# Turning the merged activations with VectorE blocks and transfers through memory, in place of TensorE turns

## The chip, the cores and the metric

The kernel runs on one core of a Trainium2 chip. The metric is device time in microseconds (us) for one execution. The core has five engines with a queue each: TensorE (PE in the profile) multiplies matrices, VectorE (DVE) and ScalarE (ACT) work elementwise, GpSimd (POOL) here does little but issue transfers, and SyncE (SP) issues the transfers of weights. Sixteen DMA engines, shared by all queues, move data between device memory and the on-chip buffer of 128 partitions. TensorE writes its results to eight accumulator banks of 128 x 512 float32.

## What is computed

One layer of a diffusion backbone over 256 tokens of 2048 features, with a prefix of 256 context tokens. The part that the change touches is the merge of two branches ahead of the output projection:

```python
def gated_merge(y_conv, y_hgrn, p_gc, p_gh, w_o):
    return (jax.nn.sigmoid(p_gc) * y_conv + jax.nn.sigmoid(p_gh) * y_hgrn) @ w_o
```

`y_conv` is a convolution branch times its pointwise weights `w_pw` (1024 x 2048), `y_hgrn` a recurrent branch times `hgrn_out_w` (1024 x 2048), and `w_o` is 2048 x 2048. Before this come a modulation, a normalisation and the input projections; behind it a normalisation, the residual and an MLP with a squared ReLU (2048 to 8192 to 2048). All of it is float32.

## The kernel before

**Products in three terms.** A float32 operand is split into a high part `hi` (rounded to the faster matmul type, `F32R`) and a low part `lo = x - hi`. A product is the sum of `hi*hi`, `hi*lo` and `lo*hi`, so three matmuls (`mm3r`, line 256, recorded at line 185). ScalarE makes the high part and VectorE the low part: lines 123 and 126 for weights, line 237 (`split`) for activations.

**The stream of weights.** `Stream` (line 52) loads tiles of 128 x 1024 (512 KB) from the SyncE queue into one of five raw buffers (`RAWS`), and prepares each (lines 123 and 126) up to four tiles (`AHEAD`) before TensorE uses it. A raw buffer is free again when VectorE has made the low part. Between the weight tiles run tiles of another product (`gemv`, line 1226): one VectorE operation, `gacc`, per tile, from the same raw buffers. In this part of the kernel one such tile goes with every two weight tiles.

**The token-major projections.** `tokens` (line 277) computes an output with tokens on partitions. Its output of 256 tokens x 2048 features is made in two groups of 1024 features, each with four accumulators: `tb` (two blocks of 128 tokens) by `j` (two blocks of 512 features). A group runs over the input features in steps `k` of 128; each step uses one weight tile and 12 matmuls. The last three steps of a group (`LAST`) are done accumulator by accumulator, so that the accumulators finish one after another, and after that each is evacuated. With `pairs=True` the order of accumulators is (tb 0, j 0), (1, 0), (0, 1), (1, 1). `pre(g, k)` is called ahead of each step of a group outside those last three.

**Around the merge.** Line 824 projects the recurrent branch (weights `who`, 8 steps in each group). Line 857 projects the convolution branch (weights `wpw`, 8 steps per group); this is "pw" below. Its evacuation `ev_pw` (line 828) merges, per token block `tb` and per block `c` of 512 features, the accumulator with the gates and the other branch: a multiplication (line 830) and an addition (line 831), both on VectorE. The merged values lie in `gp[0]`, with tokens on partitions.

The output projection (line 974, weights `wo`, 16 steps in each of two groups; "wo" below) needs them with features on partitions, as high and low part: pages `zh` and `zl`, page `c` for the features 512c to 512c + 511, in the order feature block, token. `turn_z` (line 833) makes them from 32 turns of 128 x 128 on TensorE (line 840, a transpose against an identity matrix), four to a bank, and after every four one split of the bank (128 x 512). Four of its eight steps run in pw's second group, two each at k = 3 and k = 4 (`pre_pw`); the other four in wo's first group, one each at k = 3 to 6 (`pre_wo`).

**Order.** The instructions of each engine run in the order of its queue. A scheduler fixes that order when the program is built: what stands earlier in the program has priority when it is ready, by the scheduler's own clock. `issue_after(ins)` puts instructions behind `ins` on the same engine, and nothing more; `his[-1]` and `los[-1]` are the weight splits prepared last.

**Pages.** Tiles of 128 x 1024 float32 come from one pool of 30 pages. A page is used again when its last reader is done, and an instruction that wants a new page waits for that. The loads of the residual input into `xr` (line 855, four pages of 512 KB on GpSimd's queue) and of the gain rows (lines 1276 and 1277, the same queue) take their pages from that pool, as do the gates `gp`, `zh`, `zl` and the pages of the branch activations.

Of the kernel before, what the change touches and what calls it, by code (L numbers as in the profile page):

```python
# [8 lines left out]
F32 = mybir.dt.float32  # L9
# [6 lines left out]
P = 128  # L16
T = 256
D = 2048
KT = D // P
# [7 lines left out]
TW = 1024  # L27
# [24 lines left out]
class Stream:  # L52


    def __init__(self, kn):
        self.kn = kn
        self.items = []
        self.done = 0
        self.behind = []
        self.ready = collections.deque()  # L60
        self.raws = collections.deque()
        self.dma = None
# [66 lines left out]
    def next(self, ahead=AHEAD):  # L129
        while len(self.ready) < ahead and self.done < len(self.items):  # L130
            self.prepare()
        while ahead > 1 and self.done < len(self.items) and self.items[self.done][1] is not None:
            self.prepare()
        return self.ready.popleft()


class Kernel:
    def __init__(self, ctx, tc, a, out):
        self.tc = tc
        self.nc = tc.nc  # L140
        self.a = a
        self.out = out
        self.wp = ctx.enter_context(tc.tile_pool(name="wp", bufs=1))
        self.pg = ctx.enter_context(tc.tile_pool(name="pg", bufs=1))
        self.sp = ctx.enter_context(tc.tile_pool(name="sp", bufs=1))
        self.cp = ctx.enter_context(tc.tile_pool(name="cp", bufs=1))
        self.ps = ctx.enter_context(tc.tile_pool(name="ps", bufs=1, space=bass.MemoryType.PSUM))
        self.bg = collections.deque()
        self.his, self.los = [], []
        self.credit = 0.0  # L150
        self.queued = None
# [213 lines left out]
    def run(self):  # L365
        nc, a = self.nc, self.a
# [3 lines left out]
        v = self.v  # L370
# [131 lines left out]
        for i in range(2):  # L502
            ps = self.bank()
# [160 lines left out]
        for c in range(8):  # L664
            part = sums(c, self.last3)
            ps = self.bank()
            for t in range(KP // 2):
                st.fetch_to(FETCH)
                w = st.whole()
                for k2 in range(2):  # L670
                    k = 2 * t + k2
                    g = 32 * (k % 4)
# [69 lines left out]
        for h in range(NH):  # L742
            accs = []
            for d in range(2 * (h > 0)):
                accs.append(self.bank())
                for hf in range(2):
                    hi, lo = st.next()
                    for k8 in range(8):
                        k = 8 * hf + k8
# [55 lines left out]
        gp = [[None] * 4, [None] * 4]  # L805
# [20 lines left out]
        zh, zl = self.pages(4, F32R, "zh"), self.pages(4, F32R, "zl")  # L826

        def ev_pw(tb, c, acc):
            z, y = self.cut(gp[0], tb, c), self.cut(gp[1], tb, c)
            nc.vector.tensor_tensor(z, acc, z, op=ALU.mult)  # L830
            nc.vector.tensor_tensor(z, z, y, op=ALU.add)

        def turn_z():

            for k in range(0, KT, 2):
                ps = self.bank()
                for j in range(2):
                    o = (k + j) % 8 * P
                    for tb in range(2):
                        nc.tensor.transpose(out=ps[:, j * T + tb * P:j * T + (tb + 1) * P], in_=gp[0][2 * tb + k // 8][:, o:o + P], identity=v["ident"])  # L840
                self.split(ps, self.at(zh, k, 2), self.at(zl, k, 2))
                yield
        zturn = turn_z()

        def pre_pw(g, k):
            for _ in range(2 * (g == 1 and k > 2)):
                next(zturn)

        def pre_wo(g, k):
            if g == 0 and 2 < k < 7:  # L850
                next(zturn)
            if g == 0 and 7 < k < 12:
                j = k - 8
                with self.tc.issue_after(self.los[-1].ins):
                    nc.gpsimd.dma_start(xr[j][:, :TW], a["x"][(j // 2) * P:(j // 2 + 1) * P, (j % 2) * TW:(j % 2 + 1) * TW])

        self.tokens(self.operand(self.cv), ev_pw, 1.3, nk=8, pairs=True, pre=pre_pw)


# [112 lines left out]
        hid = {}  # L972
        begun = self.first_up(yp, xr, A2, mv[:, 0], h2)
        self.tokens(zx, ev_wo, 1.4, end=True, pre=pre_wo, begin=begun)


# [243 lines left out]
    def warm(self, n=WARM):  # L1220

        ps = self.bank()
        for _ in range(n):
            self.pe(self.nc.tensor.matmul, ps[:, :P], self.ones_r, self.ones_r, start=True, stop=True)

    def gemv(self, raw, i, k, h):

        nc = self.nc
        if k == 0:
            self.accv = self.page(F32, "gacc")  # L1230
        acc = self.accv[:, :TW]
        s = self.sc[:, k:k + 1]
        if k == 0:
            nc.vector.tensor_scalar(out=acc, in0=raw, scalar1=s, scalar2=None, op0=ALU.mult)
        else:
            nc.vector.scalar_tensor_tensor(acc, raw, s, acc, op0=ALU.mult, op1=ALU.add)  # L1236
        if k == KT - 1:
            gen = self.gain_row(acc, i, h)
            self.bg.appendleft(gen)
            self.grow_gen[i, h] = gen  # L1240
# [383 lines left out]
```

## Time and profile before

| | |
|---|---|
| median of 3 runs | 1643.5 us (1642.47 to 1644.42) |
| the profiled execution, its own time | 1644.45 us |
| its span in the trace | 1642.7 us |
| memory read, written | 370.93 MB, 2.10 MB |
| granted clock of TensorE | full in all 40 slices |

The page lists busy time by engine, then 40 slices of the span, then the DMA queues, then the chain that ended last: the work followed back from the last instruction, at each step to whatever released it. What is on that chain sets the time; what is beside it has slack. Further views, asked of the same trace, are used below: the instructions of one line, the chain in order of time, busy times in chosen windows, a timeline of one engine, groups of instructions, and DMA issues. Times in the timeline and the chain are from the start of the span; pw runs at about 782 to 830 us, wo's first group from 830 us on.

### The profile page before, as it was taken

How to read it: one execution, taken by the hardware profiler on the slowest of the kernel's cores; microseconds unless marked ns; L12 is line 12 of the kernel's file. 1: busy time of each engine (PE TensorE's matmuls, PEld its weight loads, DVE VectorE, ACT ScalarE, POOL GpSimd, SP SyncE). 2: the span in 40 equal slices, each digit the busy share in tenths (PEclk: the TensorE clock that was granted, in tenths of full speed). 3: DMA queues.
4: the chain of work that ended last, by engine and by line, in shares of the span. 5: the costliest groups of instructions: out<-in, count | busy, mean ns of one | idle time of the engine just before them, and what ended most of it. 6: DMA issues, size and time to landing. Idle time of an engine off the chain costs nothing.

```text
span 1642.7 us, 22019 instructions
## 1 busy us (share of the span) xinstructions
PE 1627.8 (99%) x8211; PEld 1359.2 (83%) x8211; DVE 1163.1 (71%) x1703; ACT 799.9 (49%) x1142; POOL 8.1 (0%) x18
## 2 busy tenths in 40 slices
PE   8999999999999999999999999999999999999998
PEld 6668888888988888888888888888888888888887
DVE  7777777778868889967887766456655665566555
ACT  6553444443554444653446665445544554346543
POOL 0000000000000000000000000000000000000000
PEclk9999999999999999999999999999999999999999
DMA  9998954444656556688887376677667667666553
GB/s 375 389 395 292 318 163 149 154 142 141 204 185 227 189 187 210 228 277 294 317 291 269 136 233 204 212 237 240 219 205 232 233 214 215 232 219 195 190 192 116
DMA packets 103771, 374.47 MB, mean 228 GB/s; under 512 B 11632, under 2 KB 12400, under 8 KB 103664
## 3 DMA queue, kind: packets, MB, share of 16 engines
q1 hardware_dynamic: 102096, 368.60, 66.4%
q0 software_dynamic: 1280, 4.21, 0.9%
q8 instruction: 64, 1.05, 0.3%
q14 instruction: 43, 0.35, 0.1%
q10 hardware_dynamic: 288, 0.26, 0.0%
HBM read 370.93 MB, written 2.10 MB: 227 GB/s over the span
## 4 chain that ended last, share of the span: by engine, by line
PE 93%; DVE 2%; DMA 2%; ACT 1%; issue 1%; SPq 0%; ACTq 0%; DVEq 0%
PE bank L185 62%; PE bank L252 18%; PE bank L254 9%; PE bank L1396 2%; DMA raw<-wpw 1%; DVE wlo L126 1%; DMA x<-ctx 1%; DMA rawpage<-wm 1%; ACT whi L123 0%; PE bank L1427 0%; PE bank L1438 0%; PE bank L1436 0%; DVE gacc L1236 0%; SPq L498 0%; PE bank L1419 0%
## 5 line engine op out<-in xcount | busy, mean ns | idle before, releaser
L126 DVE TENSOR_TENSOR wlo<-raw,whi 128x1024 fp32r<-128x1024 f32 x488 | 594.7, 1224 | 356.2 <-ACT whi L123 348.4
L123 ACT ACTIVATE whi<-raw 128x1024 fp32r<-128x1024 f32 x488 | 513.4, 1059 | 577.7 <-PE bank L185 322.9
L185 PE MATMUL bank<-whi,h 128*128 128x512 f32 x1264 | 396.6, 392 | 0.8 <-ACT h L629 0.5
L252 PE MATMUL bank<-h,whi 128*128 128x512 f32 x1280 | 322.4, 394 | 0.0
L185 PEld LDWEIGHTS bank<-whi,h 128*128 128x128 f32 x1264 | 237.3, 188 | 50.9 <-DVE h L1085 0.7
L252 PEld LDWEIGHTS bank<-h,whi 128*128 128x128 f32 x1280 | 230.7, 189 | 41.3
L185 PE MATMUL bank<-wlo,h 128*128 128x512 f32 x632 | 246.9, 391 | 0.7 <-DVE wlo L126 0.5
L185 PE MATMUL bank<-whi,hidh 128*128 128x512 f32 x503 | 195.3, 388 | 0.0
L185 PE MATMUL bank<-wlo,hidh 128*128 128x512 f32 x503 | 195.3, 388 | 0.0
L185 PE MATMUL bank<-whi,hidl 128*128 128x512 f32 x503 | 195.3, 388 | 0.0
L254 PEld LDWEIGHTS bank<-h,wlo 128*128 128x128 f32 x1280 | 174.6, 190 | 12.6
L254 PE MATMUL bank<-h,wlo 128*128 128x256 f32 x1280 | 178.5, 283 | 0.0
L185 PE MATMUL bank<-h,whi 128*128 128x512 f32 x512 | 164.7, 403 | 0.0
L185 PEld LDWEIGHTS bank<-wlo,h 128*128 128x128 f32 x632 | 118.8, 188 | 26.5 <-DVE wlo L126 2.4
L185 PEld LDWEIGHTS bank<-whi,hidh 128*128 128x128 f32 x503 | 94.5, 188 | 19.3
L185 PEld LDWEIGHTS bank<-whi,hidl 128*128 128x128 f32 x503 | 94.5, 188 | 19.2
L185 PEld LDWEIGHTS bank<-wlo,hidh 128*128 128x128 f32 x503 | 94.5, 188 | 19.2
L185 PEld LDWEIGHTS bank<-h,whi 128*128 128x128 f32 x512 | 92.1, 189 | 21.4 <-issue 5.9
L185 PE MATMUL bank<-h,wlo 128*128 128x512 f32 x256 | 100.2, 391 | 0.0
L1236 DVE SCALAR_TENSOR_TENSOR gacc<-raw,silu_c,gacc 128x1024 f32<-128x1024 f32 x60 | 76.8, 1279 | 0.0
L1249 DVE SCALAR_TENSOR_TENSOR raw<-raw,silu_row 128x1024 f32<-128x1024 f32 x64 | 76.5, 1220 | 0.0
L185 PEld LDWEIGHTS bank<-h,wlo 128*128 128x128 f32 x256 | 48.1, 188 | 10.5 <-DVE wlo L126 0.3
(246 smaller groups left out, 1363.0 us busy)
## 6 DMA issues: line engine op xcount, KB each, us to landing
raw<-w SPq DMA_DIRECT2D x256, 512.0 KB, 4.3
raw<-wi SPq DMA_DIRECT2D x172, 512.0 KB, 4.4
raw<-wmt SPq DMA_DIRECT2D x64, 512.0 KB, 4.3
raw<-wm SPq DMA_DIRECT2D x64, 512.0 KB, 4.5
rawpage<-wm SPq DMA_DIRECT2D x48, 512.0 KB, 8.8
raw<-wo SPq DMA_DIRECT2D x32, 512.0 KB, 4.7
raw<-wmd SPq DMA_DIRECT2D x16, 512.0 KB, 8.6
raw<-who SPq DMA_DIRECT2D x16, 512.0 KB, 5.1
```

The costliest lines, as they stand in the source:

```text
L123: kn.his.append(nc.scalar.activation(out=hi, in_=raw, func=AF.Copy))
L126: kn.los.append(nc.vector.tensor_tensor(lo, raw, hi.bitcast(F32), op=ALU.subtract))
L185: ins = fn(*args, **kw)
L252: nc.tensor.matmul(bank, w[0][:, cut(i)], x(k)[2], start=(k == 0), stop=False)
L254: nc.tensor.matmul(bank[:, T:], w[1][:, cut(i)], x(k)[0], start=False, stop=(k == nk - 1))
L1236: nc.vector.scalar_tensor_tensor(acc, raw, s, acc, op0=ALU.mult, op1=ALU.add)
L1249: nc.vector.scalar_tensor_tensor(raw, raw, 1.0, self.srow, op0=ALU.mult, op1=ALU.mult, accum_out=self.dot[:, 32 * j + b:32 * j + b + 1])
L1396: nc.tensor.matmul(ps[:, b * P:(b + 1) * P], w, r, start=True, stop=True)
```

## The change

The turns on TensorE go. After each merge VectorE transposes the 128 x 512 block in squares of 32 x 32 into a page `zt[c]`, so that within each square features lie on partitions and tokens along the row; which square belongs to which group of 32 partitions is not yet right. When both token blocks of a page are in, `swapped` writes the page to device memory (512 KB) and reads it back with four transfers of 128 KB, which put the partition groups in place: each takes runs of 1 KB into 32 partitions. All five transfers are on GpSimd's queue. `turn_z` then only splits: eight splits of 128 x 512 from the page read back, with an access pattern that puts the runs of 32 tokens in order. Two of them run in pw's second group at k = 4, the other six in wo's first group at k = 0, 1, 5, 6, 8 and 9, behind the last prepared weight on ScalarE and VectorE.

```diff
+        self.dr = ctx.enter_context(tc.tile_pool(name="dr", bufs=1, space=bass.MemoryType.DRAM))
...
             nc.vector.tensor_tensor(z, z, y, op=ALU.add)
+            if tb == 0:
+                zt.append(self.page(F32, "turned"))
+            o = zt[c][:, :TW].rearrange("p (j u b r) -> p u b j r", j=4, u=2, b=4)[:, tb]
+            nc.vector.transpose(out=o, in_=z.rearrange("p (b j r) -> p b j r", b=4, j=4))
+            if tb:
+                zback.append(self.swapped(zt[c]))
+        zt, zback = [], []
...
-            for k in range(0, KT, 2):
-                ps = self.bank()
-                for j in range(2):
-                    o = (k + j) % 8 * P
-                    for tb in range(2):
-                        nc.tensor.transpose(out=ps[:, j * T + tb * P:j * T + (tb + 1) * P], in_=gp[0][2 * tb + k // 8][:, o:o + P], identity=v["ident"])
-                self.split(ps, self.at(zh, k, 2), self.at(zl, k, 2))
-                yield
+            for c in range(4):
+                for tb in range(2):
+                    x = zback[c].rearrange("p (i u b r) -> p u b i r", i=4, u=2, b=4)[:, tb]
+                    hi, lo = (pages[c][:, :TW].rearrange("p (b u i r) -> p u b i r", b=4, u=2, i=4)[:, tb] for pages in (zh, zl))
+                    with self.tc.issue_after(self.his[-1].ins), self.tc.issue_after(self.los[-1].ins):
+                        self.split(x, hi, lo)
+                    yield
...
-            for _ in range(2 * (g == 1 and k > 2)):
-                next(zturn)
+            if g == 1 and k == 4:
+                for _ in range(2):
+                    next(zturn)
...
-            if g == 0 and 2 < k < 7:
+            if g == 0 and k in (0, 1, 5, 6, 8, 9):
                 next(zturn)
...
+    def swapped(self, page):
+        nc = self.nc
+        there = self.dr.tile([P, TW], F32, name="there", tag="there", bufs=4)
+        nc.gpsimd.dma_start(there, page[:, :TW])
+        back = self.page(F32, "back")[:, :TW]
+        for j in range(4):
+            nc.gpsimd.dma_start(back[32 * j:32 * j + 32].rearrange("c (i f) -> c i f", i=4),
+                                there[:, j * T:(j + 1) * T].rearrange("(i c) f -> c i f", i=4))
+        return back
```

## The prediction

> **What bounds the kernel now.** I read the page from the top: busy times, then the clock, then the chain that ended last.
>
> ```profile
> span 1642.7 us, 22019 instructions
> PE 1627.8 (99%) x8211; PEld 1359.2 (83%) x8211; DVE 1163.1 (71%) x1703; ACT 799.9 (49%) x1142; POOL 8.1 (0%) x18
> ...
> PEclk9999999999999999999999999999999999999999
> ...
> PE 93%; DVE 2%; DMA 2%; ACT 1%; issue 1%; SPq 0%; ACTq 0%; DVEq 0%
> ```
>
> TensorE is busy 99% of the span at a full granted clock and makes 93% of the chain, so a matmul taken away should be worth its pace, wherever nothing else is late. But 7% of the chain is elsewhere, and the change lies in one such place. Next come the 32 turns themselves (the view of line L840), then the chain in order of time around them.
>
> ```profile
> L840 PE MATMUL bank<-pack,gate x32: 270/272/273, 814.4 to 848.3; 128*128 128x128 f32 x32
> ...
> 800.85 1.23 DVE wlo L126
> 802.08 0.61 DVE gate L830
> ...
> 812.97 1.30 DVE gacc L1236
> 814.27 0.02 issue
> 814.28 6.71 DMA raw<-wpw
> ...
> 822.19 1.24 DVE wlo L126
> ...
> 823.47 15.07 PE bank L185 x65
> 838.54 0.44 PE bank L840 x4
> 838.98 2.78 PE bank L185 x12
> 841.76 0.44 PE bank L840 x4
> ```
>
> The turns fall into two halves. The first 16 (814 to 819 us, second group of the pointwise projection, "pw") are not in this chain at all: from 800.85 to 814.27 it runs through VectorE (low parts of weights, the merges L830 and L831, `gacc`), then through one weight load of 6.71 us, then back to TensorE at 823.47. The other 16 (838 to 848 us, first group of the output projection, "wo") stand in a stretch that is TensorE alone; each block of four costs 0.44 us there.
>
> The window table in 5 us steps says how full VectorE and the DMA engines are. Columns: TensorE, its weight loads, VectorE, ScalarE, GpSimd, each busy us (instructions), the clock, DMA share, GB/s.
>
> ```profile
> 805.00:810.00 5.00, 5.00 (x23) 4.12 (x22) 4.96 (x6) 2.22 (x3) 0.53 (x1) 1.00 0.59 186
> 810.00:815.00 5.00, 5.00 (x26) 4.17 (x26) 5.00 (x7) 2.13 (x3) 1.04 (x2) 1.00 0.88 340
> 815.00:820.00 5.00, 5.00 (x30) 4.26 (x29) 3.92 (x5) 1.31 (x3) 0.00 (x0) 1.00 0.93 354
> 820.00:825.00 5.00, 4.86 (x22) 3.69 (x21) 4.04 (x5) 3.93 (x5) 0.00 (x0) 1.00 0.93 346
> 825.00:830.00 5.00, 5.00 (x24) 4.12 (x23) 4.93 (x7) 0.94 (x1) 0.00 (x0) 1.00 0.81 263
> 830.00:835.00 5.00, 5.00 (x24) 4.14 (x23) 4.96 (x7) 2.02 (x3) 0.00 (x0) 1.00 0.50 168
> 835.00:840.00 5.00, 5.00 (x26) 4.15 (x25) 5.00 (x5) 2.72 (x3) 0.00 (x0) 1.00 0.88 305
> ```
>
> VectorE is at 4.9 to 5.0 of 5 us in exactly the two stretches where the change gives it more. The two waits of TensorE near the turns, the second at the end of that chain:
>
> ```profile
> 798.55 0.50 PE L185 MATMUL bank<-wlo,h 128*128 128x512 f32 x1 [0.54 <-DVE wlo L126]
> ...
> 823.47 0.19 PEld L185 LDWEIGHTS bank<-wlo,h 128*128 128x128 f32 x1 [0.57 <-DVE wlo L126]
> ```
>
> **The change, part by part.**
>
> *Turns removed.* 32 at a pace of 0.44/4 = 0.11 us are 3.5 us of TensorE time. In pw the 16 removed (1.8 us) shorten nothing, because the chain passes beside them: TensorE only waits longer for the weights that come at 823.43. In wo the 16 removed save 4 x 0.44 = **1.8 us**. The Trainium skill, "TensorE: Matmul & The Clock Gate", Part 4, gives about 275 ns for one turn inside a kernel, dominated by the memory's latency. By that figure the saving would be 32 x 0.275 = 8.8 us. The row above agrees on the duration (272 ns), but four of them take 0.44 us of the chain, so they overlap; the full duration is a rival below.
>
> *Block transposes added on VectorE.* Eight, 128x512 each, one after every merge. None is in the trace. The nearest rows of the same size:
>
> ```profile
> L831 DVE TENSOR_TENSOR gate<-gate 128x512 f32<-128x512 f32 x8 | 5.5, 691 | 0.2
> ...
> L1500 DVE TENSOR_REDUCE lnred<-lnsq 128x256 f32<-128x1024 f32 x2 | 4.0, 2018 | 0.0
> ...
> L925 DVE TENSOR_SCALAR y<-xr,rtok 128x512 f32<-128x512 f32 x4 | 1.9, 484 | 0.0
> ...
> 817.63 1.29 DVE L237 TENSOR_TENSOR zl<-bank,zh 128x512 fp32r<-128x512 f32 x2
> ```
>
> The low end is the one-input operation, 484 ns; the high end the strided reduction, 2018 ns for 1024 elements, so 1.0 us for 512. I take the plain 512-element operation, 0.69 us, whose pace behind another is 0.61 us (the merge in the chain). Four of them fall between 802 and 814 us. They are older in program order than the low parts of weights and the `gacc` step behind them on VectorE, whose raw buffers the SyncE queue waits for before it issues the load that is late at 814.28. So the chain grows by 4 x 0.61 = **2.4 us** (1.6 to 4.0 by the two ends; nothing, if the scheduler puts them behind). The low/high splits of turned data that leave k = 3 (two at 817.63) don't shorten it: they come after 814.27.
>
> *The trip through memory.* Per page of 512 KB one write and four reads of 128 KB on GpSimd's queue, 4.2 MB in all, in 806 to 860 us. Prices: what that queue loads now, and the nearest loads of weights, first in this stretch, then in the full stretch at the start.
>
> ```profile
> xr<-x POOLq DMA_DIRECT2D x4, 512.0 KB, 5.9
> ...
> DMA packets 5201, 18.88 MB, mean 295 GB/s; under 512 B 602, under 2 KB 602, under 8 KB 5196
> ...
> raw<-wi SPq DMA_DIRECT2D x18, 512.0 KB, 9.9
> ...
> DMA packets 15996, 58.09 MB, mean 363 GB/s; under 512 B 1769, under 2 KB 1769, under 8 KB 15985
> ...
> 812.71 0.55 POOL L1277 DMA_DIRECT2D gain<-gain  x1
> ```
>
> The first packet line is for 806 to 870 us (mean 295 GB/s), the second for 0 to 160 us (363). The 64 us between hold 68 GB/s x 64 us = 4.4 MB of room: the 4.2 MB just fit on the whole, but not everywhere. At 815 to 825 us the share is 0.93 already, and the late load of 814.28 shares the engines with the first page's reads and the second page's write, about 1 MB. If all of that is ahead of it, it is 1.05 MB / 363 GB/s = 2.9 us later; if none, 0. In 805 to 815 there is room, and the 512 KB gain row of 812.71 that lies beside that load today may move away: I take **1.0 us**.
>
> Is the data back in time? First page: merged and transposed by 802.1 + 6 x 0.61 = 806, write landed by 812, four issues at 0.55 us each, reads landed near 820; its splits stand behind the preparation of weights k = 6, which is done when the row of 822.19 begins. Second: write at 815, back at 828, used from 830. No stall at 5.9 us a landing. GpSimd's queue keeps its order: a write waits behind the four reads of the page before, which wait for their write. The loads of `xr` and of the gain row are behind them too; both are used only after wo's first group, tens of us later. Pages are the other resource: `xr` waits for freed pages today.
>
> ```profile
> 789.94 0.53 POOL L855 DMA_DIRECT2D xr<-x  x1 [6.31 <-DVE gacc L1279]
> ```
>
> Eight more pages are wanted. If those that free up go to the new pages first, the `xr` loads move from 783-806 to after 812: 1.5 MB leave the stretch before the chain and join the busy one. The first could remove the 0.54 us that TensorE waits at 798; the second costs as above. I count both at nothing and keep them for the range.
>
> *Second group's merges and the earlier splits.* VectorE's rows after 826 us:
>
> ```profile
> 828.90 0.69 DVE L831 TENSOR_TENSOR gate<-gate 128x512 f32<-128x512 f32 x1
> ...
> 834.90 1.22 DVE L126 TENSOR_TENSOR wlo<-raw,whi 128x1024 fp32r<-128x1024 f32 x1
> 836.04 0.69 DVE L831 TENSOR_TENSOR gate<-gate 128x512 f32<-128x512 f32 x1
> ```
>
> VectorE gets four transposes (2.4 us) and the second page's two splits, now at wo k = 0 and 1 (1.2 us): 3.6 us before the low part of k = 3, which ends at 836.1 and is needed at 838.5. That cover of 2.4 us is gone, so up to 1.2 us of stall, none if TensorE's own delay gives VectorE the time: **1.0 us**. ScalarE has room (2 to 2.7 of 5 us), and the eight splits themselves only move.
>
> *Sum:* 2.4 + 1.0 - 1.8 + 1.0 = +2.6 us. The profiled run took 1644.45 us (1.75 us around its span of 1642.7), so 1647.05 on its scale. That run lies 0.95 us over the median of 1643.5, and against the median the sum gives **1646.1 us**.
>
> **Rivals.**
>
> *Hidden (25%).* The new VectorE work falls behind the preparation of weights, the chain of 801 to 823 us stays, and only the 1.8 us of wo are saved: 1641.7 us. With the moved `xr` loads and no stall at 798 and 823 (0.5 and 0.6 us) also the pw half counts: 1643.5 - 3.5 - 1.1 = 1638.9 us. For it: weights k = 1 and 2 are older in program order and may go first. Against it: what frees the late load's buffers is younger than the transposes.
>
> *Turns at their full duration (4%).* 32 x 0.272 = 8.7 us, 1634.8 us. Here each turn costs the duration in its row. Against it stand the four in 0.44 us and the pw half beside the chain.
>
> *Slower: the trip is late for the third and fourth page (21%).* Its place is wo k = 8 and 12.
>
> ```profile
> 840.00:845.00 5.00, 5.00 (x26) 4.11 (x25) 4.28 (x5) 2.60 (x3) 0.00 (x0) 1.00 1.00 365
> ...
> 848.61 40.83 PE bank L185 x180
> ```
>
> The merges of the second group end today near 829.6 (third page) and 836.7 us (fourth). With transposes, the third is written at 831; at 5.9 us per landing it is back at 845, the fourth, queued behind it, at 853. TensorE's step is 40.83/15 = 2.72 us (180 matmuls are 15 steps); k = 6 starts at 848.6, so k = 8 at 854 and k = 12 at 865. At 9.9 us, as in the full stretch, the third is back at 853, the fourth at 865. The 3.4 us by which pw ends later move both sides alike; with the 1.8 us saved and some 2 us (two pairs of splits) ahead of use, the fourth is about 4 us too late, and its waiting splits hold ScalarE and VectorE, with the next weights queued behind them: 1646.1 + 4 = 1650 us. It decides from about 8.5 us a landing. For it: shares of 0.88 and 1.00 at 835 to 845, reads in pieces of 1 KB. Against it: 5.9 us for `xr`. A rule speaks for it: by the Trainium skill, "SBUF — State Buffer", Two separate sides, a DMA issued from GpSimd can't write its descriptors while VectorE runs in a mode that uses both ports. The `xr` loads landed in 5.9 us beside a full VectorE, so no run here shows it; by that rule the landings would be longer, toward this rival.
>
> **How the numbers follow.** Forecast 50%, on its own 1643.5 to 1649.5 us. What can be told from no change is 0.2%, 3.3 us, so 1640.2 to 1646.8 is "same". The forecast gives 0.33 to same and 0.17 to slower; the hidden case 0.17 to same and 0.08 to faster; full duration 0.04 to faster; the late trip 0.21 to slower. Together faster 0.12, same 0.50, slower 0.38. The range goes from 1640.0 to 1651.5: it leaves out the full duration, the best of the hidden case and half of the late trips, about 0.18.
>
> **What would show it.** In the profile after: no L840 on TensorE; the chain between 800 and 830 us still through VectorE and a wpw load, some 2 to 3 us longer, with transposes in it and an idle of TensorE of 4 to 6 us in all before pw ends (the removed turns turn into waiting); a block transpose near 0.7 us; wo's first steps on TensorE alone; landings of 6 to 7 us. Wrong would be: TensorE without a gap in pw (hidden), a transpose over 1 us, or ScalarE waiting on the returned page for several us at wo k = 8 or 12 (late trip).

## The result and the profile after

| | median | runs | over before |
|---|---|---|---|
| before | 1643.41 us | 4 | |
| after | 1655.23 us (1651.44 to 1656.1) | 4 | ratio 1.0067, 95% interval 1.0054 to 1.008 |

The change makes the kernel slower by 11.0 us by the ratio (8.9 to 13.1). The forecast of 1646.1 us and its range up to 1651.5 are both too low. The profiled execution after took 1656.1 us.

The page of the kernel after, the lines that answer to those of before (in it line 186 is the matmul that was line 185, 238 the split, 831 and 832 the merge, 836 the transpose, 1256 `gacc`):

```profile
span 1654.3 us, 22006 instructions
...
PEclk9999999999999999999989999999999999999999
...
PE 89%; DMA 5%; DVE 4%; ACT 1%; issue 1%; SPq 0%; ACTq 0%; DVEq 0%
```

The 32 turns are gone and the span is longer. TensorE's share of the chain fell from 93% to 89%, transfers and VectorE took the rest, and one slice of 40 (827 to 868 us) shows a lower clock. The loss lies in that slice and in the 12 us ahead of it: the gain row's matmuls begin at 889.27 us before and at 900.65 after, so 11.4 us have gone by then. The table of windows, with the columns of the prediction's table, says where:

```profile
815.00:820.00 5.00, 4.40 (x20) 3.32 (x18) 2.51 (x2) 1.38 (x2) 0.00 (x0) 1.00 1.01 305
820.00:825.00 5.00, 3.24 (x6) 1.40 (x6) 3.99 (x6) 3.14 (x5) 2.18 (x4) 0.69 1.02 414
825.00:830.00 5.00, 4.09 (x10) 3.26 (x11) 3.79 (x4) 0.43 (x1) 0.00 (x0) 0.50 1.04 225
830.00:835.00 5.00, 5.00 (x19) 4.04 (x18) 3.75 (x6) 1.09 (x2) 0.56 (x1) 0.79 0.68 265
...
845.00:850.00 5.00, 1.11 (x5) 0.57 (x4) 2.66 (x4) 2.12 (x2) 0.00 (x0) 0.92 1.01 375
850.00:855.00 5.00, 2.28 (x5) 1.82 (x6) 3.82 (x5) 2.62 (x4) 4.32 (x8) 0.50 1.02 343
855.00:860.00 5.00, 5.00 (x21) 4.08 (x20) 3.01 (x4) 1.58 (x2) 1.05 (x2) 0.90 1.03 250
```

Add up what TensorE's column lacks of 5.00: 0.60 + 1.76 + 0.91 in 815 to 830 and 3.89 + 2.72 in 845 to 855, 9.9 us idle. The kernel before is 0.7 us short of its 80 us in 780 to 860 (79.32 busy). The clock adds to that: busy time times what the clock column lacks of 1.00, over these seven rows, is 1.0 + 2.0 + 1.1 + 0.1 + 1.1 + 0.5 = 5.8 us. So 9.2 + 5.8 - 3.5 (the 32 turns at 0.11 us that TensorE no longer does) = 11.5 us, which is the 11.4 of the landmark. The timeline of TensorE names the waits behind it (start, busy, what, and in brackets the idle time before it and who ended it):

```profile
820.46 0.50 PE L186 MATMUL bank<-whi,h 128*128 128x512 f32 x1 [1.06 <-ACT whi L123]
821.72 0.67 PE L186 MATMUL bank<-wlo,h 128*128 128x512 f32 x1 [0.76 <-DVE wlo L126]
825.91 0.80 PE L186 MATMUL bank<-wlo,h 128*128 128x512 f32 x1 [1.34 <-DVE wlo L126]
852.72 0.80 PE L186 MATMUL bank<-whi,zh 128*128 128x512 f32 x1 [6.61 <-ACT zh L238]
```

Three waits are for weights, at the end of pw. The fourth, the longest, is for the split of a page that came back from memory: the second page, at wo k = 4. Was its data late? The issue of its reads on GpSimd's queue:

```profile
822.50 2.18 POOL L1242 DMA_DIRECT2D back<-there  x4 [8.43 <-DMA there<-turned]
```

Issue to landing of all 16 reads, in the view of the tile `back`:

```profile
DMA to landing us min/median/max: 5.3/6.6/9.2
```

ScalarE's queue ahead of that split:

```profile
845.07 1.06 ACT L123 ACTIVATE whi<-raw 128x1024 fp32r<-128x1024 f32 x1 [4.37 <-DVE wlo L126]
848.69 1.06 ACT L123 ACTIVATE whi<-raw 128x1024 fp32r<-128x1024 f32 x1 [2.56 <-DVE gacc L1256]
851.09 1.06 ACT L123 ACTIVATE whi<-raw 128x1024 fp32r<-128x1024 f32 x1 [1.35 <-DVE wlo L126]
852.06 1.66 ACT L238 ACTIVATE zh<-back 128x512 fp32r<-128x512 f32 x3
```

No. The last of the four reads was issued at 824.1, and these four took 6.5 to 6.6 us, so the page was there by 831. Its split stands on ScalarE behind the high parts of three later weights (k = 5 to 7), each of which waits 1.4 to 4.4 us, and starts only when these are done, 21 us later. TensorE needs the split before those weights. The program's `issue_after(his[-1])` doesn't ask for this: it ties the page's two splits behind the weights of k = 2 and 3 only. The rest of the order is the scheduler's, made when the program was built. So the question is why weights are late, and the transfers are one answer (DMA issues at 806 to 870 us; the last number is the median from issue to landing). Before:

```profile
raw<-wo SPq DMA_DIRECT2D x20, 512.0 KB, 4.9
```

After:

```profile
raw<-wo SPq DMA_DIRECT2D x15, 512.0 KB, 7.2
...
back<-there POOLq DMA_DIRECT2D x16, 128.0 KB, 6.6
xr<-x POOLq DMA_DIRECT2D x4, 512.0 KB, 13.5
```

And the window rows above show that this isn't bytes alone: with the DMA share at 1.0 or more the engines move 414 GB/s at 820, but 225 and 250 in the stretches of 825 and 855 us, little more than half as much. (The 305 and 343 of 815 and 850 us say less: the kernel before has 325 at a share of 0.99, at 795 us.)

The other answer is VectorE, since SyncE issues a load only when VectorE has freed a raw buffer. Four pieces of the chain in order of time (start, length, what):

```profile
807.36 7.21 DMA raw<-wpw
...
817.02 7.25 DMA raw<-wo
...
832.05 1.22 DVE turned L836 x2
...
852.06 0.62 ACT zh L238
```

From 797 to 824 us the chain goes from one weight load to the next, with the splitting of weights and `gacc` between; the first four transposes are not on it. From 830 to 852 us it is on VectorE and ScalarE, and 2.0 us of it are transposes of the second group. But the loads of the three weights that hold the split landed only 0.1 to 0.4 us before their high parts began, so there the loads and VectorE end together, and this trace can't part them.

### The profile page after: what moved, and what is told of

Read it like the earlier page. It is cut to its first block, busy times and chain, and to the rows that moved or that the text cites. A ratio compares the mean times of both kernels' runs of the same rounds, so it can differ in the third digit from the quotient of the medians.

```text
span 1654.3 us, 22006 instructions
## 1 busy us (share of the span) xinstructions
PE 1629.9 (99%) x8179; PEld 1358.5 (82%) x8179; DVE 1168.7 (71%) x1711; ACT 799.6 (48%) x1142; POOL 19.1 (1%) x38
## 3 DMA queue, kind: packets, MB, share of 16 engines
q8 instruction: 64, 1.05, 0.2%
## 4 chain that ended last, share of the span: by engine, by line
PE 89%; DMA 5%; DVE 4%; ACT 1%; issue 1%; SPq 0%; ACTq 0%; DVEq 0%
PE bank L186 58%; PE bank L253 18%; PE bank L255 9%; PE bank L1416 2%; DMA rawpage<-wm 2%; DVE wlo L126 1%; DMA raw<-wpw 1%; DMA raw<-wf 1%; ACT whi L123 1%; DMA x<-ctx 1%; DVE gacc L1256 1%; DMA raw<-wo 0%; PE bank L1447 0%; PE bank L1458 0%; PE bank L1456 0%
```

## The experiments

Theory: the loss is the trip, since its reads hold the DMA engines for longer than their bytes say, the weights come late, and the order on ScalarE passes that on to the returned page. Rivals: the transposes on VectorE; the moved `xr` loads; the clock alone; the number of DMAs or the 1 KB runs. Costs in us are the ratio's part over 1 times 1643.5, with the 95% interval of the ratio behind them.

### The parts of the change

**e6_transposes_only**: the kernel before with the eight transposes into new pages, the turns kept, no trip.

```diff
             nc.vector.tensor_tensor(z, z, y, op=ALU.add)
+            if tb == 0:
+                zt.append(self.page(F32, "turned"))
+            o = zt[c][:, :TW].rearrange("p (j u b r) -> p u b j r", j=4, u=2, b=4)[:, tb]
+            nc.vector.transpose(out=o, in_=z.rearrange("p (b j r) -> p b j r", b=4, j=4))
+        zt = []
```

> The kernel before, with its 32 turns, plus the eight block transposes into pages that nobody reads (no transfers). VectorE theory (the prediction's first term, four transposes on the chain ahead of the late weight load): +2.4 us or more over before, 1645.5 to 1648 us, and no drop of the granted clock. Traffic theory and queue-order theory: both need the transfers, so within 1.5 us of before (1643.4).

1649.25 us, 1.0029 (1.0016 to 1.0042): +4.8 us. But the new pages also move the `xr` loads to 805 us and later, so the next run takes the pages away.

**e7_small_transposes**: the same, written to a small scratch tile that takes no page.

```diff
+            o = self.small(512, "turned")
+            nc.vector.transpose(out=o.rearrange("p (b j r) -> p b j r", b=4, j=4), in_=z.rearrange("p (b j r) -> p b j r", b=4, j=4))
```

> The kernel before, with its turns, plus the eight block transposes into a small scratch buffer that nobody reads: the same VectorE time as the kernel with transposes into pages (which was 4.8 us over before), but no page is taken, so the loads of xr should stay at 783 to 806 us. VectorE theory (the 0.61 us each on the chain are the cost): again +4 to +5 us. Page theory (the new pages push the xr loads into 805 to 813 us, beside the late weight load): most of it gone, +0 to +2.5 us.

1647.21 us, 1.0024 (1.0014 to 1.0034): +3.9 us. So most of e6 is VectorE; the moved loads are the 0.8 us between, less than the intervals can tell. The chain in order of time of e7 passes through VectorE from the first merge to the late load:

```profile
801.10 0.61 DVE gate L830
...
802.47 0.71 DVE turned L833
...
804.52 0.72 DVE turned L833
...
810.00 0.62 DVE turned L833
...
812.91 0.30 DVE turned L833
...
815.93 5.30 DMA raw<-wpw
```

From that merge to the load are 14.8 us, where the chain before has 12.2 (802.08 to 814.28): 2.6 us more for four transposes.

**e17_first_four**: e7 with only the four of the first group.

```diff
-            nc.vector.transpose(out=o.rearrange("p (b j r) -> p b j r", b=4, j=4), in_=z.rearrange("p (b j r) -> p b j r", b=4, j=4))
+            if c < 2: nc.vector.transpose(out=o.rearrange("p (b j r) -> p b j r", b=4, j=4), in_=z.rearrange("p (b j r) -> p b j r", b=4, j=4))
```

> The kernel of e7_small_transposes with only the four block transposes of the first group of the merges (801 to 814 us), which stand ahead of the late weight load; the four of the second group are left out. All eight cost 3.9 us. If the whole cost is the first four ahead of that load, at 0.70 us each (2.8 us, with a half-clock stretch behind the longer wait on top): 1646 to 1647.5. If the first four cost what the prediction gave them, 2.4 us, and the second group's the other 1.0 to 1.5: 1645.5 to 1646.2. If they hide: 1643 to 1644.5, and the second group's are the dear ones.

1649.32 us, 1.003 (1.0019 to 1.0042): +4.9 us, not less than all eight; the intervals overlap. The four ahead of the late load account for the cost, and none of the second four shows, in this kernel without a trip. TensorE's longest wait in it:

```profile
826.09 0.50 PE L185 MATMUL bank<-wlo,h 128*128 128x512 f32 x1 [2.04 <-DVE wlo L126]
```

This profiled execution took 1647.0 us, at a mean clock of 1.000; its other six runs are at 0.998 or 0.999 and take 1647.74 to 1649.51. So some 3 us of the cost come at a full clock; the up to 2.5 more come in runs with a lower mean clock, of which there is no trace.

**e12_no_turns**: the kernel before without the 32 turns; the splits read merged values that aren't turned.

```diff
-                ps = self.bank()
-                for j in range(2):
...
-                        nc.tensor.transpose(out=ps[:, j * T + tb * P:j * T + (tb + 1) * P], in_=gp[0][2 * tb + k // 8][:, o:o + P], identity=v["ident"])
+                ps = self.cut(gp[0], 1, k // 4)
```

> The kernel before with the 32 turns left out and nothing in their place: the splits read merged pages as they lie, so the operand of the output projection is not turned and the output is not the reference's. Prediction's claim (the 16 turns of the pointwise projection lie beside the chain and save nothing, the other 16 save 0.44 us per four): 1.8 us less than before, 1641.5 to 1642.5 us. Additive theory (every turn saves its pace of 0.11 us): 3.5 us less, about 1640 us.

1642.35 us, 0.9993 (0.9984 to 1.0001): -1.2 us, 2.6 at the most. The 3.5 us of both halves are out of reach, because TensorE waits a little behind the place of pw's turns, before pw ends:

```profile
821.43 0.50 PE L185 MATMUL bank<-wlo,h 128*128 128x512 f32 x1 [0.76 <-DVE wlo L126]
823.77 0.50 PE L185 MATMUL bank<-wlo,h 128*128 128x512 f32 x1 [0.65 <-DVE wlo L126]
```

**e1_no_trip**: the kernel after, with the splits reading the transposed page at once; the squares stay where they are.

```diff
     def swapped(self, page):
...
-        return back
+        return page
```

> The changed kernel with the trip left out: the splits read the block-transposed page as it is, so the squares are not in place and the output is not the reference's. Traffic theory and queue-order theory: the loss is gone, the turns are saved, 1640 to 1643 us. VectorE theory: the chain of the second group stays longer by 2.4 us, 1644 to 1647 us.

1645.27 us, 1.0007 (0.9998 to 1.0016): +1.2 us. The trip is thus 9.9 us of the 11.0. And with a trip that cost nothing the change would gain 0.3 us over the kernel before at the most.

**e2_trip_unused**: the kernel before with transposes (as in e6) and trip, whose pages nobody reads; the turns kept.

```diff
             nc.vector.tensor_tensor(z, z, y, op=ALU.add)
...
+            if tb:
+                self.swapped(zt[c])
```

> The kernel before, with its 32 turns, plus the transposes and the whole trip through memory, whose result nobody reads. Traffic theory (4.2 MB beside the weights make them late, TensorE idles and its clock drops): 1651 us or more, weight loads landing in 7 us and more, idle of TensorE of 4 us or more between 815 and 830 us. Queue-order theory (what costs is the second page's splits behind late weights on ScalarE): no 6.6 us wait, 1646 to 1648 us. VectorE theory: as the kernel with the transposes alone.

1657.08 us, 1.0085 (1.0069 to 1.0102): +14.0 us. No split waits for a page here, so the order of returned pages on ScalarE has no part in it. TensorE's longest wait is at the turns, for a bank that an operation of VectorE (`gain_row`) has to free; that operation stands on VectorE behind the low part of a late weight. The other waits are for weights, 0.9 us at the most. And the clock drops:

```profile
821.61 1.11 PE L848 MATMUL bank<-pack,gate 128*128 128x128 f32 x4 [4.04 <-DVE gain_row L1313]
...
820.00:825.00 5.00, 3.39 (x12) 3.00 (x13) 4.37 (x7) 2.92 (x5) 2.18 (x4) 0.52 1.04 414
```

**e8_x_first**: the kernel after, with the `xr` loads moved ahead of pw in the program, out of the trip's stretch.

```diff
-            if g == 0 and 7 < k < 12:
-                j = k - 8
-                with self.tc.issue_after(self.los[-1].ins):
-                    nc.gpsimd.dma_start(xr[j][:, :TW], a["x"][(j // 2) * P:(j // 2 + 1) * P, (j % 2) * TW:(j % 2 + 1) * TW])
+
+        xr = self.pages(4, F32, "xr")
+        for j in range(4):
+            nc.gpsimd.dma_start(xr[j][:, :TW], a["x"][(j // 2) * P:(j // 2 + 1) * P, (j % 2) * TW:(j % 2 + 1) * TW])
...
```

> The changed kernel with the four xr loads moved ahead of the pointwise projection in program order, so that they get their pages first and the new pages wait. Page theory: xr lands before 810 us, not at 853 us and after; 2 MB leave the stretch with the trips, 2 to 5 us less than the change (1650 to 1653 us). Trip theory (the transfers of the trip itself hold up the weights): no gain, 1655 us or more, because the first page now also waits for its slot.

1656.11 us, 1.0076 (1.0061 to 1.0091), with a wait of 7.16 us for `zh` at 853.82. No gain: the moved loads are not the cause.

### What is dear in the trip

**e4_whole_rows**: the kernel after with one read per page, 128 rows of 4 KB, in place of four. The squares are not put in their place.

```diff
-        for j in range(4):
-            nc.gpsimd.dma_start(back[32 * j:32 * j + 32].rearrange("c (i f) -> c i f", i=4),
-                                there[:, j * T:(j + 1) * T].rearrange("(i c) f -> c i f", i=4))
+        nc.gpsimd.dma_start(back, there)
```

> The changed kernel with one transfer of 512 KB per page for the read, whole rows of 4 KB, in place of four that gather runs of 1 KB into 32 partitions each: the partition groups are not put in place, so the output is not the reference's. If the form of the reads makes the trip dear (share 1.0 at only 225 to 282 GB/s while they run): 4 us less than the change or more, 1651 us or less, and over 350 GB/s at share 1.0. If only the bytes count: as the change, 1653 to 1657 us.

1648.82 us, 1.0029 (1.0018 to 1.0041): the same bytes, and 6.2 us less than after. The shape of the reads is the larger part of the trip's cost. It changes three things at once: the partitions of a read, its runs and the number of reads. The next runs part them.

**e10_rows_by_32**: whole rows again, by four reads into 32 partitions each. The squares are not put in their place.

```diff
         for j in range(4):
-            nc.gpsimd.dma_start(back[32 * j:32 * j + 32].rearrange("c (i f) -> c i f", i=4),
-                                there[:, j * T:(j + 1) * T].rearrange("(i c) f -> c i f", i=4))
+            nc.gpsimd.dma_start(back[32 * j:32 * j + 32], there[32 * j:32 * j + 32])
```

> The changed kernel with four reads of 128 KB into 32 partitions each, as it has, but each of whole rows of 4 KB: the partition groups are not put in place, so the output is not the reference's. If runs of 1 KB make the reads dear: as with one read of whole rows, 1647 to 1650 us. If the four transfers into 32 partitions each are what is dear: as the change, 1653 to 1657 us.

1652.9 us, 1.0055 (1.0042 to 1.0069): +9.0 us, with no 1 KB runs.

**e16_rows_spread**: e10 with every fourth partition in place of a block of 32.

```diff
-            nc.gpsimd.dma_start(back[32 * j:32 * j + 32], there[32 * j:32 * j + 32])
+            nc.gpsimd.dma_start(back[j::4], there[j::4])
```

> The kernel of e10_rows_by_32 (four reads per page, each of 32 whole rows of 4 KB, so the squares are not put in their place), with one difference: the 32 partitions that a read reaches are every fourth one of the 128 in place of a block of 32. Number of DMAs, bytes and packets are those of e10_rows_by_32 (1652.9). Theory of the block of 32 partitions: near the whole-row read (1648.8), 1647.5 to 1650, with over 350 GB/s at full DMA share between 805 and 860 us. Rival, the number of DMAs (four of 128 KB in place of one of 512 KB): 1651.5 to 1654.5 as e10_rows_by_32, with stretches of 250 to 290 GB/s at full share.

1649.24 us, 1.0037 (1.0024 to 1.0049): 3.0 us less than e10 and 1.3 more than one read. The intervals of e10 and e16 overlap a little (1.0042 to 1.0049), but all four runs of e10 (1652.06 us and more) lie above all five of e16 (1650.53 and less). Windows of e10 with reads under way:

```profile
810.00:815.00 5.00, 5.00 (x24) 4.14 (x23) 4.85 (x6) 1.06 (x1) 0.56 (x1) 1.00 1.05 283
...
850.00:855.00 5.00, 5.00 (x17) 3.93 (x17) 3.22 (x5) 1.32 (x3) 1.75 (x4) 0.70 1.05 256
```

The same in e16:

```profile
820.00:825.00 5.00, 3.47 (x16) 2.55 (x15) 5.00 (x7) 1.21 (x2) 2.08 (x4) 1.00 0.98 385
...
845.00:850.00 5.00, 4.96 (x13) 3.92 (x14) 3.72 (x5) 1.05 (x3) 2.61 (x5) 0.59 1.00 397
```

The number of reads, bytes and rows are the same; what differs is which 32 partitions a read reaches, and with them which rows of the memory. In such windows full engines move 385 to 397 GB/s in e16; in e10 256 and 283 in the two shown, 370 and 334 in 820 to 830 us. What the transfers take as a whole is plainer: over 800 to 870 us GpSimd's transfers (queue q0 in the view of transfers) are 6.82 MB in both, and their packets took 30.2% of the sixteen engines' time in e10, 24.7% in e16 and 25.2% in e4. So blocks of 32 partitions are one dear thing, and the number of reads shows no price that is clear of noise. The Trainium skill, "SBUF — State Buffer", "Door 1: The DMA port swizzle", says that the pace of a transfer hangs on how many of 16 ports its partitions reach. By its formula a block of 32 partitions reaches 8, and every fourth partition reaches all 16; these rows agree.

**e13_all_rows**: the same result as after, each read spread over all 128 partitions of 256 columns.

```diff
-        for j in range(4):
-            nc.gpsimd.dma_start(back[32 * j:32 * j + 32].rearrange("c (i f) -> c i f", i=4),
-                                there[:, j * T:(j + 1) * T].rearrange("(i c) f -> c i f", i=4))
+        for i in range(4):
+            nc.gpsimd.dma_start(back[:, i * T:(i + 1) * T],
+                                there[32 * i:32 * i + 32].rearrange("c (j f) -> j c f", j=4))
```

> The kernel after, with the same eight block transposes, the same bytes, the same number of DMAs and the same 1 KB pieces; only the four reads of a page are cut the other way: each takes 32 rows of the memory and spreads them over all 128 partitions of 256 columns, in place of 32 partitions of 1024 columns. The result is the same. Theory that the cost of the trip is transfers that reach only 32 partitions: near the kernel with whole-row reads (1648.8), so 1648 to 1650.5, with 'back' landing in about 6 us, raw<-wo in 5.5 to 6.5 us and over 350 GB/s wherever the DMA share is at 1.0 between 805 and 860 us. Rival, the 1 KB pieces or the number of DMAs: within 1.5 us of the kernel after, 1653.5 to 1656.5, with 225 to 305 GB/s at full share.

1654.66 us, 1.0068 (1.0055 to 1.0081): a miss, no gain at all. All partitions are reached, but the packets have changed with it. The packets at 800 to 870 us, after:

```profile
DMA packets 6077, 21.42 MB, mean 306 GB/s; under 512 B 859, under 2 KB 859, under 8 KB 6072
```

e13:

```profile
DMA packets 7424, 20.84 MB, mean 298 GB/s; under 512 B 2351, under 2 KB 2351, under 8 KB 7419
```

Some 1500 more are small, all under 512 B (neither kernel has packets of 1 KB: as many lie under 2 KB as under 512 B), and its stretches with reads show 286, 234 and 199 GB/s at a share of 1.0. A second way of cutting the reads is as dear as the first; whether by its small packets or by how its pieces are dealt to the engines was not tried.

**e9_pieces_on_write**: the same result as after, the squares put in place on the way out: four writes from 32 partitions each, then one whole read.

```diff
-        nc.gpsimd.dma_start(there, page[:, :TW])
+        rows = there.rearrange("(j c) (i f) -> i c j f", j=4, i=4)
+        for i in range(4):
+            nc.gpsimd.dma_start(rows[i], page[32 * i:32 * i + 32, :TW].rearrange("c (j f) -> c j f", j=4))
...
+        nc.gpsimd.dma_start(back, there)
```

> The changed kernel with the work of the trip swapped, and the same result: four writes out of 32 partitions each put the runs of 1 KB in place in memory, and one read of whole rows of 4 KB brings the page back. If what is dear is the reading into 32 partitions or of short runs: as with whole rows, 1647 to 1650 us. If short runs or 32 partitions are dear on either side: as the change, 1653 to 1657 us.

1654.32 us, 1.0065 (1.0049 to 1.008): no gain in time. But the engines do move more while the second page's writes are under way (812.91 to 820 us), and TensorE's first wait, 1.05 us, comes only behind pw:

```profile
810.00:815.00 5.00, 5.00 (x23) 4.14 (x23) 5.00 (x7) 2.13 (x2) 2.09 (x4) 1.00 1.01 374
815.00:820.00 5.00, 5.00 (x23) 3.90 (x23) 3.62 (x4) 2.12 (x2) 0.09 (x1) 1.00 1.03 417
```

So transfers out of a block of 32 partitions hold the engines up less than those into it. They aren't free: GpSimd's 6.82 MB took 28.1% of the engines' time here, 25.2% in e4, which has the same reads and whole writes. For that direction these figures bear the Trainium skill's rule out only in part. What was won is lost at the second page, in the timeline of TensorE:

```profile
847.01 0.80 PE L186 MATMUL bank<-whi,zh 128*128 128x512 f32 x1 [7.58 <-ACT zh L238]
```

### The order on ScalarE, and the clock

Four kernels carry the same edit, which queues the next weight's preparation behind each returned split.

```diff
-                        self.split(x, hi, lo)
+                        self.stream.behind = [self.split(x, hi, lo)]
```

**e3_splits_first** is the kernel after with it, **e14_all_rows_first** e13, **e15_rows_first** e4 (its squares aren't in place either), **e18_write_first** e9.

> The changed kernel with one thing more: the next weight that is prepared is queued behind each split of turned data, on ScalarE and on VectorE, so that the second page's splits stand ahead of weights k = 4 and 5 of the output projection. Queue-order theory: the wait of 6.6 us at k = 4 and the half clock behind it go, about 8 us less than the change, 1646 to 1648 us. Traffic theory: weights stay late, the wait only changes its name, 1652 us or more; the idle in the second pw group (820 to 826 us) stays in both.

> The kernel of e13_all_rows, with the next weight's preparation queued behind each returned split (the edit of e3_splits_first). If what is left of the trip once its transfers are quick (about 3 to 4 us over the kernel without a trip) is the second page's splits that stand on ScalarE behind late weights, 1645.5 to 1647.5 and no wait of over 2 us of TensorE for zh. Rival, that the weights are late in any case since 4.2 MB more pass in this stretch: within 1 us of e13_all_rows, with the waits at other weights.

> The kernel of e4_whole_rows (one read of 512 KB per page, squares not put in their place), with the next weight's preparation queued behind each returned split (the edit of e3_splits_first). If what the quick trip still costs over no trip (1648.8 against 1645.3) is the order on ScalarE: 1645.5 to 1647, without the wait of about 3 us near 844. If it is the bytes in this stretch: 1648 to 1650, with TensorE's waits at weights.

> The kernel of e9_pieces_on_write (the squares put in place by four writes out of 32 partitions, then one read of 512 KB; the same result as the kernel after), with the next weight's preparation queued behind each returned split (the edit of e3_splits_first). In e9 the DMA engines moved 374 to 417 GB/s at 810 to 825 us, yet TensorE waited 7.58 us at 847 for the second page's split, and the time stayed at 1654.3. If that order is what kept it slow once the transfers are quick: 1646 to 1649, no wait of over 2 us for zh, and a smaller gain from the order with the slow reads (1.7 us in e3_splits_first) explained. Rival, the 1 KB pieces keep the weights late wherever they are: 1651.5 to 1654.5, with the waits moved to weights as in e3_splits_first.

By the ratios:

| transfers | without | with the order | gain |
|---|---|---|---|
| after (reads into blocks of 32) | 1655.23, 1.0067 | e3: 1653.6, 1.0057 (1.0042 to 1.0072) | 1.6 us |
| e13 (reads of 256 columns) | 1654.66, 1.0068 | e14: 1653.59, 1.0057 (1.0043 to 1.0071) | 1.8 us |
| e4 (one whole read) | 1648.82, 1.0029 | e15: 1646.44, 1.002 (1.0011 to 1.0029) | 1.5 us |
| e9 (placed by the writes) | 1654.32, 1.0065 | e18: 1651.03, 1.0048 (1.0034 to 1.0062) | 2.8 us |

In each row the two intervals overlap, but all four gains are of one sign. The long wait for `zh` is gone in all four. TensorE's waits at 790 to 875 us, summed by what they were for (us in total, times, longest), in e3:

```profile
PE bank L186 <- DVE wlo L126: 4.7, 5, 1.8
PE bank L186 <- ACT whi L123: 2.8, 2, 2.3
```

and in e15:

```profile
PE bank L186 <- DVE wlo L126: 2.8, 4, 1.4
PE bank L186 <- ACT whi L123: 0.9, 1, 0.9
```

With slow transfers the 6.61 us become waits for weights and little is won: the weights are late in any case, and the order only chose where TensorE waits for them. With quick ones e15 comes to 2.1 us over e1, which has no trip. e18, expected at 1646 to 1649, missed by 2 us: its weights are still late behind 835 us:

```profile
838.21 0.80 PE L186 MATMUL bank<-wlo,zh 128*128 128x512 f32 x1 [2.79 <-DVE wlo L126]
...
835.00:840.00 5.00, 2.21 (x6) 1.49 (x5) 5.00 (x8) 0.00 (x0) 2.20 (x5) 0.80 0.45 125
```

Traffic isn't the cause of this wait, with a DMA share of 0.45. VectorE has no gap from 828 to 842 us, and the low part that TensorE waits for starts at 836.95, behind the second group's merges and transposes and one returned split. No run takes these away there. e18 is the best kernel with the whole change in it, 3.1 us under after, and still slower than before.

**e5_warm**: the kernel after with 64 matmuls of 128 x 128 on a constant ahead of wo k = 4, where TensorE waits 6.61 us.

```diff
+            if g == 0 and k == 4:
+                self.warm(64)
```

> The changed kernel with 64 small matmuls on constants ahead of k = 4 of the output projection, in the place where TensorE waits 6.6 us for the second page's splits. If the half clock after a wait costs by itself (matmuls of 0.8 in place of 0.4 us until 856 us): the clock stays at 1.00 there and the time falls by 1.5 to 2 us to about 1653.5 us. If the clock does not follow from the wait: no change or, the matmuls being in the way, slower.

1653.48 us, 1.0061 (1.0046 to 1.0076): 1.0 us less by the ratios, inside the intervals. In its profile the clock stays full all through, and the wait for `zh` is 0.23 us. At a full clock that execution still took 1652.62 us, some 9 us over before, so the lower clock is a part of the loss and not its cause. That it follows the waits is shown only in part: with matmuls in the place of the long wait no drop came behind it, but the waits at the end of pw were there as well (0.76 and 2.02 us), and in this execution they brought none.

## Why the prediction was wrong

- **Turns removed, -1.8 us: right.** e12 gave -1.2 us (-2.6 to +0.2), and the pw half turned into waits as the prediction said. One turn counted at its pace and not at its duration (the rival of 1634.8 us) is excluded.
- **Transposes, +2.4 us: right without the trip, small in size.** In e7 the chain went where it was drawn, through VectorE to the late load. A transpose takes 0.70 us (eight of them, of 669 to 712 ns), and the first four lengthen the chain by 2.6 us. In all e7 measured 3.9 us; the clock was in no term of the sum. In the kernel after, the trip moved the chain: between 800 and 824 us it goes through loads, with no transpose on it, which is not the sign that was forecast. TensorE's idle before pw ends came to 3.3 us there (4 to 6 was forecast). The lower bound of the term, 1.6 us, doesn't follow from its row: 4 x 0.484 is 1.9.
- **Late transfers, +1.0 us (0 to 2.9): the step that failed.** "The 4.2 MB just fit" was reckoned at 363 GB/s, a pace of whole loads into 128 partitions. In the kernel after, full engines move as little as 225 and 250 while the trip's reads run, and a weight takes 7.2 us to land in place of 4.9. The trip costs 9.9 us (after against e1). A read in one piece takes 6.2 us of that away (e4): 3.0 are the block of 32 partitions (e10 against e16), 2.0 the 1 KB runs that put the squares in place (after against e10), and 1.3 the four reads in place of one (e16 against e4). The intervals overlap in each of the three; only between e10 and e16 do the runs themselves lie apart. Quick and in the better order, the same bytes cost 2.1 us (e15 against e1), which is near the term as predicted.
- **No stall for the data of page two: wrong by its queue.** The first page was in time, and the second was back at 831 us, 3 us later than reckoned, because its write took 8.4 us to land; "used from 830" left out that its split stands on ScalarE behind three late weights. The prediction reckoned when data lands, and not behind what its reader stands.
- **Second group, +1.0 us: open.** e17 against e7 shows no cost of the second four transposes where there is no trip. With it, 2.0 us of them lie on the chain of the kernel after ahead of the long wait, and in e18 TensorE waits 2.79 us behind such work; no run has the trip without them.
- **The late trip (21%, 1650 us)** was the nearest rival, with the landings of 6 to 7 us and splits and weights that hold each other up. But its place was pages three and four, it had the splits hold the weights, and its price was 4 us over the forecast. What came was page two, at k = 4, with late weights holding the split.
- **The clock** was full before and was counted as full after. By the sum above the lower clock adds 5.8 us in that trace. The rule of the Trainium skill that the prediction cited, that GpSimd can't write descriptors beside VectorE, got no support: the trip's issues took 0.55 us each beside a busy VectorE (2.18 us for four in the row of 822.50). Whether VectorE was in such a mode then, the trace doesn't tell.

## What to carry to other kernels

Price a transfer by its shape as well as its bytes: look in the windows for what full DMA engines move beside such transfers, and where the trace has no such shape, take a bound that is wide. Where the engines are near full, the cost shows in other queues' loads, and from there in whatever was ordered behind the work on those loads. Work taken off the busiest engine saves only the part that stands on the chain: here 1.2 of 3.5 us, and four 0.7 us operations put on the other engine's chain cost more than that (3.9 us by themselves).

## What was not expected of the hardware

- Reads into blocks of 32 partitions took 30.2% of the sixteen engines' time over 800 to 870 us, the same bytes into every fourth partition 24.7%. Beside the first, full engines moved as little as 256 GB/s, beside the second 385 to 397, beside writes out of such blocks 374 to 417.
- The granted clock fell to 0.50 after short waits of TensorE in some executions and not in others. In e4 one wait of 1.96 us was enough, by its timeline and its window (0.50 from 823.1 to about 826.5 us):

```profile
822.43 0.50 PE L186 MATMUL bank<-wlo,h 128*128 128x512 f32 x1 [1.96 <-DVE wlo L126]
```

```profile
820.00:825.00 5.00, 3.04 (x10) 2.10 (x9) 5.00 (x7) 1.37 (x2) 0.53 (x1) 0.81 0.99 371
```

In e5 two waits, 0.76 and 2.02 us within 4.5 us, left it at 1.00:

```profile
821.51 0.50 PE L186 MATMUL bank<-wlo,h 128*128 128x512 f32 x1 [0.76 <-DVE wlo L126]
825.25 0.50 PE L186 MATMUL bank<-wlo,h 128*128 128x512 f32 x1 [2.02 <-DVE wlo L126]
```

```profile
820.00:830.00 10.00, 7.20 (x29) 4.90 (x28) 9.66 (x13) 3.35 (x5) 2.18 (x4) 1.00 1.03 327
```

In e17 0.44 and 2.04 us left it at 1.00 too; in e1 1.84 and 0.76 us brought it down. So neither the longest wait nor their sum tells the two apart, and what does is open. The Trainium skill, "TensorE: Matmul & The Clock Gate", "Why this matters for your kernels", asks for no idle gap over some 3 us. Here gaps of under 2 us sometimes cost the clock too.
